# Seven-product blocks of a feed-forward layer in a new interleaving, with two sums per step left to accumulating transfers

## The chip, the cores and the metric

The kernel runs on one core of one Trainium2 chip. The time is device microseconds (us) of that core for one execution of the whole program; the kernel before has a median of 1907.07 us over three runs (1906.84 to 1908.11). The engines are named as the profile names them: PE (TensorE, matmuls), PEld (its weight loads), DVE (VectorE), ACT (ScalarE), POOL (GpSimd) and SP (SyncE, which here only issues transfers). Each engine takes its instructions strictly in the order in which they stand in its queue.

## The reference

Two layers work on 256 tokens of width 2048 in float32. Each layer has a first part (a projection, a gated unit, windowed attention and an output projection) and then a feed-forward part of width 5632:

```
D_FF = -(-8 * D_MODEL // (3 * 256)) * 256
...
        x = x + mixed @ w_out[l]
        h2 = rms_norm(x, norm2_g[l])
        x = x + (jax.nn.silu(h2 @ w_gate[l]) * (h2 @ w_up[l])) @ w_down[l]
```

Only the products with `w_gate` and `w_up` are touched by the change.

## The kernel before

**Exact products from split operands.** Every weight tile comes from HBM as float32, 128 partitions by 1024 elements (512 KB, a `raw` tile). `split2` (L117) makes two tiles of it: ACT casts it to `wh` (L123), and DVE subtracts that from the original, which gives `wl` (L124). `mm3` (L158) then issues three matmuls for each 128-row piece: high by high, high by low, low by high (L159 to L161). There are eight `raw` buffers, five of `wh` and four of `wl`. A `raw` buffer is free for the next load only when its last reader is done.

**Two streams of units.** The feed-forward part has eleven column blocks of 512. Ten of them (`S_BLOCKS`) are computed by `seven` (L338): the two token halves, two row parities of the weights and the pair (gate, up) form a two by two product, done with seven products in place of eight. One of these handles one `raw` tile and six matmuls at a time, called a half unit here. A block has four steps `i` over the rows, seven half units in each, so 28 half units. Beside them runs the plain stream: the eleventh block and the down projection, in full units of one `raw` tile and twelve matmuls (`unit`, L163). The loop at the end of `trunk` takes them in turn: it goes through 300 yields of the seven-product stream per layer and slips in the full units of the plain stream at an even rate, 83 of them over those yields, so about 8.3 full units for each block. The rest of the plain stream follows alone.

**The operands.** With B11 and B21 the two row parities of the gate weights and B12 and B22 those of the up weights, the seven products read: (one) B11; (two) B21, added to the same bank as one; (three) B22; (five) B11+B12; (six) B11+B12+B22, the tile `t2`; (seven) B12+B22; (four) `t2`+B21, added to the bank of seven. Five PSUM banks m0 to m4 hold the partial results of a block, and a few adds of 128x512 (m0, c21, c12, c22) join them.

**How the sums are made before.** In each step `i` the kernel loads B11, B12 and B22 together. DVE adds B12 onto B11 (L365) and makes `t2` (L366). B12+B22 is made for steps 0 and 2 by an accumulating transfer that POOL issues (L368: it reads B22 from HBM again and adds it onto the tile B12), for steps 1 and 3 by DVE (L372). B21 is added onto `t2` by another accumulating transfer (L374). In the second phase B21 is loaded once more as the operand of product two.

**What sets the order.** The Python code is traced in program order, and a list scheduler then decides in which order the instructions stand on each engine. It may move an instruction ahead of others of its engine when nothing it depends on forbids it; `tc.issue_after(x)` keeps instructions behind `x` on their engine. The order is fixed when the program is built.

Of the kernel before, what the change touches and what calls it, by code (L numbers as in the profile page):

```python
# [12 lines left out]
F32 = mybir.dt.float32  # L13
# [57 lines left out]
EXT_AT = (6.5, 8, 11, 13, 16, 18, 21.5, 24)  # L71
MASK_AFTER = ((5, 5), (4, 4))
GATE_LOAD = ((24, 29), (5, 15))
PARTS = (
    "a0 a0 a1 a1 s a0 a0 s a1 s a1 s s s b0 s b0 s b0 s b0 s b1 s b1 s b1 s b1 s b2 b2 b2 b2 b3 b3 b3 b3",
    "a0 a0 a1 a1 a0 a0 s a1 a1 s b0 b0 s b0 s b0 s s b1 s b1 s b1 s b1 s s b2 s b2 s b2 b2 s b3 b3 b3 b3",
# [14 lines left out]
def trunk(ctx, tc, x, xt, w_in, w_q, w_out, w_oa, w_uh, w_gate, w_up, w_down, sgu_w, sgu_g, consts,  # L91
# [66 lines left out]
    def mm3(acc, ah, al, wh, wl, first, last, again=False):  # L158
        nc.tensor.matmul(acc, ah, wh, start=first, stop=False, skip_group_check=again)  # L159
        nc.tensor.matmul(acc, ah, wl, start=False, stop=False, skip_group_check=again)  # L160
        nc.tensor.matmul(acc, al, wh, start=False, stop=last, skip_group_check=again)  # L161
# [171 lines left out]
    def seven(src, pairs, ext, out, end=lambda sg: None, soon=False, by_dma=(), put_off=False):  # L333
        bank = [pa.tile([P, NB], F32, tag="acc", name=f"m{i}") for i in range(5)]

        def s_unit(raw, m, i, op, first, last):
            wh, wl = split2(raw)
            for j in range(2):  # L338
                ah, al = (op(2 * i + j, h) for h in range(2))
                mm3(  # L340
                    bank[m], ah, al, wh[:, j, :], wl[:, j, :], first and j == 0,
                    last and j == 1, m in (0, 2),
                )
            tick(0.5)

        def a_op(k, t):
            return lambda p, h: pairs[p][:, h, k, t * P : (t + 1) * P]

        def e_op(n):
            return lambda p, h: ext[p][:, h, n, :]  # L350

        kept = []
        before = []
        for i in range(4):
            b11 = raw_load(src(0, 0, i))
            b12 = raw_load(src(0, 1, i))
            b22 = raw_load(src(1, 1, i))
            t2 = ap.tile([P, 2, NB], F32, tag="spt", name="t2", bufs=4)
            first, last = i == 0, i == 3
            s_unit(b11, 0, i, a_op(0, 0), first, last)  # L360
            yield
            if soon and first:
                s_unit(b22, 4, i, e_op(3), first, last)
                yield
            nc.vector.tensor_tensor(b11, b11, b12, ALU.add)  # L365
            nc.vector.tensor_tensor(t2, b11, b22, ALU.add)  # L366
            if i in by_dma:
                nc.gpsimd.dma_start(b12, src(1, 1, i), accum_op=ALU.add)  # L368
            s_unit(b11, 1, i, e_op(1), first, last)
            yield  # L370
            if i not in by_dma:
                nc.vector.tensor_tensor(b12, b12, b22, ALU.add)  # L372
            s_unit(t2, 3, i, e_op(2), first, last)
            anchor[0] = nc.gpsimd.dma_start(t2, src(1, 0, i), accum_op=ALU.add)  # L374
            yield
            if before:
                s_unit(*before.pop())
                yield
            if not (soon and first):
                s_unit(b22, 4, i, e_op(3), first, last)  # L380
                yield
            kept.append(t2)
            if put_off and i in by_dma and not last:
                before.append((b12, 2, i, e_op(0), first, last))
                continue
            s_unit(b12, 2, i, e_op(0), first, last)
            yield
        m0, c12, c21, c22 = (
            zp.tile([P, NB], F32, tag="z", name=v) for v in ("m0", "c12", "c21", "c22")
        )  # L390
        nc.scalar.copy(m0, bank[0])
        nc.vector.tensor_tensor(m0, bank[3], m0, ALU.add)
        yield

        def add(out, x, y):
            nc.vector.tensor_tensor(out, x, y, ALU.add)

        steps = {
            0: lambda: add(c21, bank[2], m0),
            1: lambda: (nc.scalar.copy(bank[2], c21), add(c12, bank[1], m0)),  # L400
            2: lambda: (add(c22, bank[1], c21), add(c12, bank[4], c12)),
            5: lambda: out(0, bank[0], m0, c12),
        }
        for i in range(8):
            if i < 4:
                s_unit(raw_load(src(1, 0, i)), 0, i, a_op(1, 0), False, i == 3)
            else:
                s_unit(kept[i - 4], 2, i - 4, a_op(1, 1), False, i == 7)
            yield
            steps.get(i, lambda: None)()  # L410
        later(1, lambda: out(1, bank[2], c21, c22))
        end([m0, c21])
        yield

    def seven_low(src, pairs, ext, done, tag="hT"):
        def half(raw, acc, op, i, first=False, stop=False):
            wh, wl = split2(raw)
            for j in range(2):
                ah, al = (op(2 * i + j, h) for h in range(2))
                mm3(  # L420
                    acc, ah, al, wh[:, j, :], wl[:, j, :], first and i + j == 0,
                    stop and i + j == 2, not first,
                )
            tick(0.5)

        def a_op(k, t):
            return lambda p, h: pairs[p][:, h, k, t * P : (t + 1) * P]

        def e_op(n):
            return lambda p, h: ext[p][:, h, n, :]  # L430

        def bank(name):
            return pa.tile([P, NB], F32, tag="acc", name=name)

        def held(name):
            return tp.tile([P, 2, NB], F32, tag=tag, name=name)

        x, y, s = [], [], []
        acc0 = bank("l0")
# [12 lines left out]
        nc.scalar.copy(acc1, acc0)  # L452
        for i in range(2):
            half(s[i], acc1, e_op(2), i, False, True)
            anchor[0] = nc.gpsimd.dma_start(s[i], src(1, 0, i), accum_op=ALU.add)
            yield
        mp = wp.tile([P, 2, NB], F32, tag="raw", name="mp", bufs=8)
        nc.scalar.copy(mp[:, 0], acc1)
        acc2 = bank("l2")
        for i in range(2):  # L460
            half(y[i], acc2, e_op(0), i, True, True)
            yield
        nc.scalar.copy(mp[:, 1], acc2)
        for i in range(2):
            half(raw_load(src(1, 0, i)), acc0, a_op(1, 0), i, False, True)
            yield
        done[0, 0](acc0, None)
        for i in range(2):
            half(x[i], acc1, e_op(1), i, False, True)
            yield  # L470
        done[1, 1](acc1, mp[:, 1])
        for i in range(2):
            half(s[i], acc2, a_op(1, 1), i, False, True)
            yield
        done[0, 1](acc2, mp[:, 0])
        for i in range(2):
            half(raw_load(src(1, 1, i)), acc1, e_op(3), i, False, True)
            yield
        done[1, 0](acc1, None)

    def q_product(lay, pairs, ext):
        q = {"k": 0}
        q["steps"] = seven(
            lambda r, c, i: w_q[lay, c, i, r], pairs, ext, lambda *a: q["out"](*a),
            soon=True, by_dma=range(4 if lay == 0 else 0),
        )
        return q

    def q_to(q, share):
# [32 lines left out]
    for lay in range(L):  # L522
# [526 lines left out]
        def act_later(b, sg, held=held, release=release):  # L1049
            for c in range(2):  # L1050
                def ready(c=c):
                    held.append((b, c, sg))
                    release()

                later(2 + c, ready)
# [3 lines left out]
            nc.vector.scalar_tensor_tensor(sg, c, nrstd2[t], sg, ALU.mult, ALU.mult)  # L1059

        def s_block(b, lay=lay, pairs2=pairs2, ext2=ext2, gated=gated, act_later=act_later):
            return seven(
                lambda r, c, i: (w_gate, w_up)[c][lay, b, i, r], pairs2, ext2, gated,
                lambda sg: act_later(b, sg), soon=b == S_BLOCKS[0], by_dma=(0, 2), put_off=True,
            )

        seven_done = [False]

        def s_stream(s_block=s_block):
            for b in S_BLOCKS:  # L1070
                yield from s_block(b)

        seeds = []
        left = [NFF]
# [230 lines left out]
```

## Time and profile before

| what | value |
|---|---|
| median of three runs | 1907.07 us |
| the profiled execution, its time | 1906.77 us |
| its span, first to last instruction | 1905.1 us |
| PE busy | 1892.9 us (99%) |
| DVE busy | 1745.5 us (92%) |
| ACT busy | 1374.7 us (72%) |
| POOL busy | 183.9 us (10%) |
| granted TensorE clock | 1.000 |

The first layer's seven-product stream runs from about 300 to 940 us of the span, the second's from about 1250 to 1855 us. The stretches from 370 to 860 us and from 1310 to 1800 us lie wholly inside, and each covers eight blocks. A row of the group view gives the line, engine, operation, output and inputs, shapes and count, then busy time and the mean of one in ns, then the idle time of the engine just before these instructions and what ended it. A row of the wait view gives the waiting engine and line, whom it waited for, the total in us, how many times and the longest. In the views PEld's waits are PE's: a matmul follows its weight load.

### The profile page before, as it was taken

How to read it: one execution, taken by the hardware profiler on the slowest of the kernel's cores; microseconds unless marked ns; L12 is line 12 of the kernel's file. 1: busy time of each engine (PE TensorE's matmuls, PEld its weight loads, DVE VectorE, ACT ScalarE, POOL GpSimd, SP SyncE). 2: the span in 40 equal slices, each digit the busy share in tenths (PEclk: the TensorE clock that was granted, in tenths of full speed). 3: DMA queues.
4: the chain of work that ended last, by engine and by line, in shares of the span. 5: the costliest groups of instructions: out<-in, count | busy, mean ns of one | idle time of the engine just before them, and what ended most of it. 6: DMA issues, size and time to landing. Idle time of an engine off the chain costs nothing.

```text
span 1905.1 us, 25218 instructions
## 1 busy us (share of the span) xinstructions
PE 1892.9 (99%) x8624; PEld 1544.2 (81%) x8624; DVE 1745.5 (92%) x1894; ACT 1374.7 (72%) x1860; POOL 183.9 (10%) x184
## 2 busy tenths in 40 slices
PE   9999999999999999999999999999999999999999
PEld 6887788888888888888888778888888888888887
DVE  7988989999999999999798888999999999999993
ACT  8668777677767776777776886766877677676774
POOL 0231001000100001000002200000000100010000
PEclk9999999999999999999999999999999999999999
DMA  9973668888977897889578648697789788888783
GB/s 356 261 284 133 194 202 243 248 247 276 271 238 245 270 290 228 243 261 290 185 217 291 191 153 237 212 280 224 233 282 288 227 254 264 270 249 251 249 277 110
DMA packets 129153, 463.12 MB, mean 243 GB/s; under 512 B 14336, under 2 KB 14720, under 8 KB 129024
## 3 DMA queue, kind: packets, MB, share of 16 engines
q1 hardware_dynamic: 105840, 378.54, 53.9%
q0 software_dynamic: 22464, 81.80, 23.7%
q8 instruction: 67, 1.10, 0.2%
q10 hardware_dynamic: 720, 1.18, 0.2%
q14 instruction: 62, 0.51, 0.1%
HBM read 459.36 MB, written 2.10 MB: 242 GB/s over the span
## 4 chain that ended last, share of the span: by engine, by line
PE 94%; ACT 2%; DVE 2%; issue 1%; DMA 0%; POOL 0%; SPq 0%; DVEq 0%; ACTq 0%; POOLq 0%
PE m L160 15%; PE m L159 15%; PE m L161 15%; PE dacc L160 11%; PE dacc L159 11%; PE dacc L161 11%; PE acc L160 4%; PE acc L161 3%; PE acc L159 3%; PE l L159 1%; PE l L160 1%; PE l L161 1%; PE ps_f L242 1%; PE ps_n L242 1%; DVE wl L124 1%
## 5 line engine op out<-in xcount | busy, mean ns | idle before, releaser
L123 ACT CAST wh<-raw 128x1024 fp32r<-128x1024 f32 (+1 forms) x794 | 814.0, 1050 | 366.5 <-DVE raw L365 165.7
L124 DVE TENSOR_TENSOR wl<-raw,wh 128x1024 fp32r<-128x1024 f32 (+1 forms) x794 | 943.9, 1217 | 83.0 <-issue 25.5
L159 PE MATMUL m<-wh,ext 128*128 128x512 f32 x704 | 276.7, 393 | 0.0
L160 PE MATMUL m<-wl,ext 128*128 128x512 f32 x704 | 275.0, 391 | 0.0
L161 PE MATMUL m<-wh,ext 128*128 128x512 f32 x704 | 274.4, 390 | 0.0
L160 PE MATMUL dacc<-wl,aT 128*128 128x512 f32 x624 | 243.5, 390 | 0.0
L159 PE MATMUL dacc<-wh,aT 128*128 128x512 f32 x624 | 243.0, 391 | 0.0
L161 PE MATMUL dacc<-wh,aT 128*128 128x512 f32 x624 | 242.9, 389 | 0.0
L124 DVE TENSOR_TENSOR wl<-t,wh 128x1024 fp32r<-128x1024 f32 x176 | 213.1, 1221 | 10.0 <-issue 5.2
L123 ACT CAST wh<-t 128x1024 fp32r<-128x1024 f32 x176 | 184.3, 1051 | 37.0 <-DVE t L366 14.1
L159 PE MATMUL m<-wh,hT 128*128 128x512 f32 x528 | 206.3, 391 | 0.0
L160 PE MATMUL m<-wl,hT 128*128 128x512 f32 x528 | 205.7, 390 | 0.0
L161 PE MATMUL m<-wh,hT 128*128 128x512 f32 x528 | 205.5, 389 | 0.0
L160 PEld LDWEIGHTS m<-wl,ext 128*128 128x128 f32 x704 | 132.2, 188 | 29.1 <-DVE wl L124 2.2
L159 PEld LDWEIGHTS m<-wh,ext 128*128 128x128 f32 x704 | 132.2, 188 | 27.6 <-ACT wh L123 0.8
L161 PEld LDWEIGHTS m<-wh,ext 128*128 128x128 f32 x704 | 132.1, 188 | 27.5
L159 PEld LDWEIGHTS dacc<-wh,aT 128*128 128x128 f32 x624 | 117.1, 188 | 25.0 <-ACT wh L123 0.7
L160 PEld LDWEIGHTS dacc<-wl,aT 128*128 128x128 f32 x624 | 117.2, 188 | 24.7 <-DVE wl L124 0.6
L161 PEld LDWEIGHTS dacc<-wh,aT 128*128 128x128 f32 x624 | 117.1, 188 | 24.2
L374 POOL DMA_DIRECT2D t<-in_w_gate_dram x80 | 69.1, 864 | 525.0 <-DVE wl L124 412.9
L161 PEld LDWEIGHTS m<-wh,hT 128*128 128x128 f32 x528 | 99.1, 188 | 20.6
L159 PEld LDWEIGHTS m<-wh,hT 128*128 128x128 f32 x528 | 99.1, 188 | 20.3
(212 smaller groups left out, 2907.5 us busy)
## 6 DMA issues: line engine op xcount, KB each, us to landing
raw<-in_w_gate_dram SPq DMA_DIRECT2D x176, 512.0 KB, 5.9
raw<-in_w_up_dram SPq DMA_DIRECT2D x176, 512.0 KB, 5.9
raw<-in_w_down_dram SPq DMA_DIRECT2D x176, 512.0 KB, 5.8
t<-in_w_gate_dram POOLq DMA_DIRECT2D x80, 512.0 KB, 7.7
raw<-in_w_in_dram SPq DMA_DIRECT2D x68, 512.0 KB, 6.7
raw<-in_w_out_dram SPq DMA_DIRECT2D x48, 512.0 KB, 4.3
raw<-in_w_up_dram POOLq DMA_DIRECT2D x40, 512.0 KB, 6.5
raw<-in_w_q_dram SPq DMA_DIRECT2D x32, 512.0 KB, 5.7
```

Source lines behind the costliest of these rows:

```text
L123: nc.scalar.copy(wh[:, j : j + step, :], src)
L124: last_wl[0] = nc.vector.tensor_tensor(wl[:, j : j + step, :], src, f(wh[:, j : j + step, :]), ALU.subtract)
L159: nc.tensor.matmul(acc, ah, wh, start=first, stop=False, skip_group_check=again)
L160: nc.tensor.matmul(acc, ah, wl, start=False, stop=False, skip_group_check=again)
L161: nc.tensor.matmul(acc, al, wh, start=False, stop=last, skip_group_check=again)
L242: nc.tensor.transpose(ps[:, j, t * P : (t + 1) * P], blocks[t][:, j * P : (j + 1) * P], ident)
L374: anchor[0] = nc.gpsimd.dma_start(t2, src(1, 0, i), accum_op=ALU.add)
```

## The change

A class `Lean` replaces `seven` for the ten feed-forward blocks of each layer; the query projection keeps `seven`. Its half units are the same seven products over the same four steps, but each product is a method that handles one step, and a table `LEAN` says when. Row m of the table has the places of product m+1 for the steps 0 to 3; block n is shifted by 28 places. The places of a block run to 37, so a block's last half units lie between the first ones of the next.

```diff
+LEAN = (
+    (0, 4, 8, 12), (24, 26, 27, 29), (6, 10, 14, 18), (30, 31, 33, 37), (7, 11, 15, 19),
+    (16, 20, 22, 23), (13, 17, 21, 25),
+)
...
+        def onto(self, dst, i):
+            anchor[0] = nc.gpsimd.dma_start(dst, self.src(0, 1, i), accum_op=ALU.add)
+
+        def one(self, i):
+            self.raw[1, i] = raw_load(self.src(0, 0, i))
+            self.half(1, self.raw[1, i], i)
+            self.onto(self.raw[1, i], i)
+
+        def three(self, i):
+            self.raw[3, i] = raw_load(self.src(1, 1, i))
+            self.half(3, self.raw[3, i], i)
+
+        def five(self, i):
+            self.half(5, self.raw[1, i], i)
+            self.t2[i] = ap.tile([P, 2, NB], F32, tag="spt", name="t2", bufs=4)
+            with tc.issue_after(last_wl[0].ins):
+                self.add(self.t2[i], self.raw[1, i], self.raw[3, i])
+            self.onto(self.raw[3, i], i)
+
+        def six(self, i):
+            if i == 0:
+                nc.scalar.copy(self.acc(3), self.bank[0])
+            self.half(6, self.t2[i], i)
...
+        def two(self, i):
+            b21 = raw_load(self.src(1, 0, i))
+            self.half(2, b21, i)
+            self.add(self.t2[i], self.t2[i], b21)
...
+                nc.scalar.copy(z["m0"], bank[3])
+            elif i == 1:
+                self.add(z["c21"], bank[2], z["m0"])
+            elif i == 2:
+                nc.scalar.copy(bank[2], z["c21"])
+                self.add(z["c12"], bank[1], z["m0"])
...
+    def lean_run(blocks):
+        steps = sorted(
+            (28 * n + LEAN[m][i], n, m, i) for n in range(len(blocks)) for m in range(7) for i in range(4)
+        )
+        for _, n, m, i in steps:
+            b = blocks[n]
+            (b.one, b.two, b.three, b.four, b.five, b.six, b.seven)[m](i)
+            yield
+            if m in (3, 5) and i == 3:
+                yield
...
         def s_stream(s_block=s_block):
-            for b in S_BLOCKS:
-                yield from s_block(b)
+            return lean_run([s_block(b) for b in S_BLOCKS])
```

B12 is no longer loaded as a tile. Two accumulating transfers per step add it onto B11 (after product one has been split) and onto B22 (after `t2` has been made). `t2` is still made by DVE. B21 is no longer added onto `t2` by a transfer that reads it a second time: DVE adds the tile that product two loads anyway. The bank of product six starts from a copy of m0 by ACT, in place of DVE's later add of the two banks (L392 before). Over both layers the program has 80 plain loads fewer on SP (176 of `w_up` become 96), 40 accumulating transfers more on POOL (120 become 160), 40 additions of 128x1024 fewer on DVE (the 120 of L365 and L372 go, 80 onto `t2` come), 20 additions of 128x512 fewer on DVE and 20 copies of 128x512 more on ACT. The number of matmuls is the same. Outside the two seven-product streams the order on PE is the same as before.

Three places show how the order moved. The first is DVE in the first layer around the transposes of a finished block (`aT` are the transposed results). `raw` are loaded tiles, the number tells the buffers of the text apart. Before:

```order
L1038 TENSOR_TENSOR aT_5033<-ps_f_5028,aT_5033 128x512
L365 TENSOR_TENSOR raw_5083<-raw_5083,raw_5085 128x1024
L366 TENSOR_TENSOR t2_5089<-raw_5083,raw_5087 128x1024
L124 TENSOR_TENSOR wl_5103<-raw_5083,wh_5102 128x1024
L372 TENSOR_TENSOR raw_5085<-raw_5085,raw_5087 128x1024
L1038 TENSOR_TENSOR aT_5070<-ps_f_5065,aT_5070 128x512
L124 TENSOR_TENSOR wl_5114<-t2_5089,wh_5113 128x1024
```

Now, at the same stage of a block of the first layer:

```order
L128 TENSOR_TENSOR wl_5682<-raw_5537,wh_5681 128x1024
L453 TENSOR_TENSOR t2_5691<-raw_5537,raw_5651 128x1024
L128 TENSOR_TENSOR wl_5697<-t2_5516,wh_5696 128x1024
L1141 TENSOR_TENSOR aT_5648<-ps_f_5643,aT_5648 128x512
L128 TENSOR_TENSOR wl_5707<-raw_5560,wh_5706 128x1024
L128 TENSOR_TENSOR wl_5719<-raw_5716,wh_5718 128x1024
L453 TENSOR_TENSOR t2_5516<-t2_5516,raw_5841 128x1024
L128 TENSOR_TENSOR wl_5737<-raw_5734,wh_5736 128x1024
```

Before, DVE made three sums in a row for one step. Now it makes one, `t2_5691`; and the sum onto `t2_5516`, which reads the tile `raw_5841` of product two, stands behind `t2_5691` with four rows between, thirteen DVE rows ahead of the split of that same tile (`wl_5844`).

The second place is SP at the loads that belong to these rows. Before:

```order
L112 DMA raw_5083<-in_w_gate_dram 128x1024
L112 DMA raw_5085<-in_w_up_dram 128x1024
L112 DMA raw_5087<-in_w_up_dram 128x1024
L112 DMA raw_5130<-in_w_down_dram 128x1024
L112 DMA raw_5178<-in_w_gate_dram 128x1024
```

Now:

```order
L116 DMA raw_5560<-in_w_up_dram 128x1024
L116 DMA raw_5578<-in_w_down_dram 128x1024
L116 DMA raw_5619<-in_w_gate_dram 128x1024
L116 DMA raw_5651<-in_w_up_dram 128x1024
L116 DMA raw_5663<-in_w_down_dram 128x1024
L116 DMA raw_5716<-in_w_down_dram 128x1024
L116 DMA raw_5734<-in_w_up_dram 128x1024
L116 DMA raw_5779<-in_w_down_dram 128x1024
L116 DMA raw_5823<-in_w_down_dram 128x1024
L116 DMA raw_5841<-in_w_gate_dram 128x1024
```

Before, the three tiles of a step come together. Now they come one by one. When DVE has made `t2_5691` and so given back `raw_5537`, the tiles 5560, 5619, 5651, 5716, 5734, 5779 and 5823 of this list are still wanted or still to come, seven of the eight buffers, and `raw_5841` is the next to be loaded.

More of the change, by code (lines that the diff above doesn't have):

```diff
@@ L413, in seven, with __init__, a_op, e_op @@
         yield
+    class Lean:
+        def __init__(self, src, pairs, ext, out, end=lambda sg: None):
+            self.src, self.out, self.end = src, out, end
+            self.bank, self.raw, self.t2, self.z = {}, {}, {}, {}
+            def a_op(k, t):
+                return lambda p, h: pairs[p][:, h, k, t * P : (t + 1) * P]
+            def e_op(n):
+                return lambda p, h: ext[p][:, h, n, :]
+            self.home = {
+                1: (0, a_op(0, 0)), 2: (0, a_op(1, 0)), 3: (4, e_op(3)), 4: (2, a_op(1, 1)),
+                5: (1, e_op(1)), 6: (3, e_op(2)), 7: (2, e_op(0)),
+            }
+        def acc(self, m):
+            if m not in self.bank:
+                self.bank[m] = pa.tile([P, NB], F32, tag="acc", name=f"m{m}")
+            return self.bank[m]
+        def half(self, n, raw, i):
+            m, op = self.home[n]
+            wh, wl = split2(raw)
+            first, last = n in (1, 3, 5, 7) and i == 0, i == 3
+            for j in range(2):
+                ah, al = (op(2 * i + j, h) for h in range(2))
+                mm3(
+                    self.acc(m), ah, al, wh[:, j, :], wl[:, j, :], first and j == 0,
+                    last and j == 1, m in (0, 2, 3),
+                )
+            tick(0.5)
+        def add(self, out, x, y):
+            nc.vector.tensor_tensor(out, x, y, ALU.add)
+        def onto(self, dst, i):
[17 more added lines that the diff above has]
+            self.half(6, self.t2[i], i)
+        def seven(self, i):
+            self.half(7, self.raw[3, i], i)
+        def two(self, i):
+            b21 = raw_load(self.src(1, 0, i))
+            self.half(2, b21, i)
+            self.add(self.t2[i], self.t2[i], b21)
+            z, bank = self.z, self.bank
+            if i == 0:
+                for v in ("m0", "c12", "c21", "c22"):
+                    z[v] = zp.tile([P, NB], F32, tag="z", name=v)
+                nc.scalar.copy(z["m0"], bank[3])
[4 more added lines that the diff above has]
+                self.add(z["c12"], bank[1], z["m0"])
+            else:
+                self.add(z["c22"], bank[1], z["c21"])
+                self.add(z["c12"], bank[4], z["c12"])
+        def four(self, i):
+            self.half(4, self.t2[i], i)
+            z, bank = self.z, self.bank
+            if i == 0:
+                self.out(0, bank[0], z["m0"], z["c12"])
+            elif i == 3:
+                later(1, lambda: self.out(1, bank[2], z["c21"], z["c22"]))
+                self.end([z["m0"], z["c21"]])
@@ L415, in seven_low @@
+    def lean_run(blocks):
+        steps = sorted(
+            (28 * n + LEAN[m][i], n, m, i) for n in range(len(blocks)) for m in range(7) for i in range(4)
+        )
+        for _, n, m, i in steps:
[4 more added lines that the diff above has]
+                yield
     def seven_low(src, pairs, ext, done, tag="hT"):
@@ L482, in q_product @@
         q = {"k": 0}
[L483 to L486, printed above, removed]
+        args = (lambda r, c, i: w_q[lay, c, i, r], pairs, ext, lambda *a: q["out"](*a))
+        q["steps"] = seven(*args, soon=True, by_dma=range(4 if lay == 0 else 0))
         return q
@@ L1061, in s_block @@
         def s_block(b, lay=lay, pairs2=pairs2, ext2=ext2, gated=gated, act_later=act_later):
-            return seven(
+            return Lean(
                 lambda r, c, i: (w_gate, w_up)[c][lay, b, i, r], pairs2, ext2, gated,
-                lambda sg: act_later(b, sg), soon=b == S_BLOCKS[0], by_dma=(0, 2), put_off=True,
+                lambda sg: act_later(b, sg),
             )
```

## The prediction

> **What bounds the kernel now.** I read the engines' busy time in the seven-product stretches first, then PE's waits there, then what DVE and the transfers do under them.
>
> The windows view: the first layer's start of this part, then 370 to 860 us (first layer) and 1310 to 1800 us (second), each eight blocks long:
>
> ```profile
> core 0: us, PE busy (x) PEld busy (x) DVE busy (x) ACT busy (x) POOL busy (x), PEclk, DMA share, GB/s
> 252.00:300.00 48.00, 48.00 (x224) 39.70 (x224) 42.58 (x64) 32.44 (x53) 2.46 (x3) 1.00 0.66 205
> ...
> 370.00:860.00 490.00, 490.00 (x2191) 403.95 (x2190) 470.80 (x441) 349.35 (x409) 40.63 (x47) 1.00 0.84 258
> ...
> 1310.00:1800.00 490.00, 490.00 (x2189) 403.73 (x2188) 470.80 (x442) 351.94 (x411) 41.53 (x48) 1.00 0.84 258
> ```
>
> PE is the bound: 490.00 of 490. DVE stands close behind with 96%, ACT has 71%, the transfers 84%. A block takes 490/8 = 61.25 us, a matmul 490/2191 = 0.224 us, so a half unit (six) 1.34 us and a full unit 2.68 us. Since the number of matmuls stays, the change can gain only what PE still waits. A busy PE may hide waits, so I take them from the wait view of PE's weight loads, 300 to 940 us and then 1250 to 1860 us:
>
> ```profile
> PEld ps_f L242 <- DVE aT L1038: 1.5, 4, 0.4
> PEld m L160 <- DVE wl L124: 1.0, 4, 0.4
> PEld dacc L159 <- ACT wh L123: 0.4, 1, 0.4
> PEld m L159 <- ACT wh L123: 0.3, 1, 0.3
> PEld dacc L160 <- DVE wl L124: 0.3, 1, 0.3
> PEld ps_f L242 <- DVE c L1059: 0.3, 1, 0.3
> ```
>
> ```profile
> PEld ps_f L242 <- DVE aT L1038: 1.4, 4, 0.4
> PEld m L160 <- DVE wl L124: 0.8, 3, 0.4
> PEld m L159 <- ACT wh L123: 0.5, 2, 0.3
> PEld dacc L159 <- ACT wh L123: 0.4, 1, 0.4
> PEld dacc L160 <- DVE wl L124: 0.3, 1, 0.3
> PEld ps_f L242 <- DVE c L1059: 0.2, 1, 0.2
> ```
>
> Here is the whole prize. The splits (wl and wh rows) make PE wait 2.0 us in each layer, 4.0 in all; the transposes that wait for DVE (ps_f rows) 1.8 and 1.6, 3.4 in all. Together 7.4 us, 0.39% of the time. No removal of DVE work can give more than this.
>
> **The change part by part. DVE's work.** DVE's groups between 370 and 860 us, eight blocks:
>
> ```profile
> L124 DVE TENSOR_TENSOR wl<-raw,wh 128x1024 fp32r<-128x1024 f32 x224 | 265.4, 1220 | 10.8 <-issue 4.1 <-ACT wh L123 4.0 <-PE dacc L160 1.0
> L124 DVE TENSOR_TENSOR wl<-t,wh 128x1024 fp32r<-128x1024 f32 x63 | 76.1, 1221 | 4.2 <-issue 2.2 <-ACT wh L123 1.4
> L365 DVE TENSOR_TENSOR raw<-raw 128x1024 f32<-128x1024 f32 x32 | 39.2, 1224 | 0.9
> L366 DVE TENSOR_TENSOR t<-raw 128x1024 f32<-128x1024 f32 x32 | 39.1, 1223 | 0.9
> L372 DVE TENSOR_TENSOR raw<-raw 128x1024 f32<-128x1024 f32 x15 | 18.3, 1217 | 0.0
> L392 DVE TENSOR_TENSOR m<-m,m 128x512 f32<-128x512 f32 x8 | 5.5, 686 | 0.6 <-PE m L161 0.6
> ```
>
> Gone are L365, L372 and L392: 39.2 + 18.3 + 5.5 = 63.0 us. Four additions of B21 per block come, 32 in this stretch; the trace has none, but L366 is the same operation on the same kinds of tile: 39.1 us. Net 23.9 us less of 470.8. DVE's idle time goes from 490 - 470.8 = 19.2 to 43.1 us, from 2.4 to 5.4 us per block: 96% busy becomes 91%, and the reserve doubles.
>
> **ACT and PSUM.** ACT gets 20 copies, of the kind of these rows of the page:
>
> ```profile
> L400 ACT COPY m<-c 128x512 f32<-128x512 f32 x22 | 12.9, 588 | 5.3 <-DVE c L396 5.1
> L391 ACT COPY m<-m 128x512 f32<-128x512 f32 x22 | 12.7, 576 | 0.0
> ```
>
> 20 x 0.58 = 11.6 us over 1,220 us, hidden in ACT's idle time (140.65 of 490 us); without that cover it would cost these 11.6 us. The chain from product seven's last step over c21 (0.69, as L392) and its copy (0.59) to product four has, by the order, five half units between on PE at the narrowest, 6.7 us. With three splits queued ahead on DVE (3.66) it needs 4.9, so I put it at nothing.
>
> **The transfers.** The DMA view of 370 to 860 us, and SP's own waits there:
>
> ```profile
> q1 hardware_dynamic: 27691, 100.85, 54.3%
> q0 software_dynamic: 6912, 25.17, 29.4%
> ...
> raw<-in_w_down_dram SPq DMA_DIRECT2D x65, 512.0 KB, 5.7
> raw<-in_w_up_dram SPq DMA_DIRECT2D x64, 512.0 KB, 6.0
> raw<-in_w_gate_dram SPq DMA_DIRECT2D x63, 512.0 KB, 6.3
> t<-in_w_gate_dram POOLq DMA_DIRECT2D x31, 512.0 KB, 7.6
> raw<-in_w_up_dram POOLq DMA_DIRECT2D x16, 512.0 KB, 6.7
> ```
>
> ```profile
> SPq L112 <- DVE wl L124: 409.7, 192, 6.6
> ```
>
> A load costs 54.3% of 490 us over 192, 1.39 us of all 16 engines; an accumulating transfer 29.4% of 490 over 47, 3.07 us. A block loses four of the first and gains two of the second: +0.6 us, 84% becomes 85%. So the transfers get no relief though they move fewer bytes. POOL is busy 40.63 of 490 us and takes two more issues per block easily. The accumulated sums are read six or seven places of the table later. At the narrowest, four half units and two full ones lie between on PE, 4 x 1.34 + 2 x 2.68 = 10.7 us; they land in 6.7 to 7.6 us, and with ACT's cast are in time:
>
> ```profile
> L123 ACT CAST wh<-raw 128x1024 fp32r<-128x1024 f32 x223 | 228.5, 1052 | 107.4 <-DVE raw L365 65.2 <-PE dacc L161 22.5 <-PE m L161 10.2
> ```
>
> 7.6 + 1.05 is under 10.7. I put this at nothing; the third rival below has what it costs otherwise. Only the first block of a layer has nothing interleaved: there product five of step 0 follows its product one after three half units and one full unit, 6.7 us, where landing and cast need 7.8 to 8.7. That is 1.1 to 2.0 us short, once per layer, and the lead of the splits may cover it: bounds 0 and 4.0 us for both layers; I take 0.7, nearer to nothing, since PE is busy 48.00 of 48 us from 252 to 300 us, where that block starts, and DVE there only 42.58: the splits can be ahead.
>
> **The new wait.** The sum onto `t2` on DVE now reads a loaded tile long before that tile's own split, and nothing queued behind it on DVE (the next splits, and PE after them) can pass. SP waits 192 times for 192 loads above: every load goes out when a buffer comes free. In the piece of order shown, `raw_5841` can go out when `t2_5691` is done, and DVE has four rows until it needs it: three splits and a 128x512 operation as in L392, 3 x 1.22 + 0.69 = 4.3 us. The load takes 6.3 (the w_gate row). DVE then stands still for 2.0 us. Through the order of a layer, sixteen of the forty such sums have 3.7 to 6.1 us of DVE rows between the release and the sum, 82.5 us in all; the others have 7.3 or more. At 6.3 us they cost 16 x 6.3 - 82.5 = 18.3 us of DVE per layer, 1.8 per block. The order before has no such place: DVE has at least 8.5 us of rows between release and first use.
>
> DVE's stall is PE's only where it exceeds the splits' lead. There are four `wl` buffers, so DVE can be three units ahead of the one on PE, 4.0 us in half units; a mean stall of 18.3/16 = 1.1 us fits in. For the few of 2 us and more at a moment of little lead I put 1.0 us over both layers; bounds are 0 and what the rival below gives.
>
> **The sum.** DVE's free reserve is 5.4 - 1.8 = 3.6 us per block where it was 2.4. The waits for splits (4.0) could go wholly or stay; I take half off, -2.0. The waits for transposes (3.4) hang on DVE too, but also on the one bank that is handed back and forth; half, -1.7. New stalls +1.0, first blocks +0.7: -2.0. The profiled execution took 1906.77 us, 1.7 outside its span of 1905.1; it becomes 1904.8, and from the median of 1907.07, 0.3 above it, **1905.1 us**.
>
> **The rivals.** *The load decides (slower).* If the loads behind the sixteen sums take 7.6 us, as the slower accumulating transfers do, DVE stalls 16 x 7.6 - 82.5 = 39.1 us per layer, 3.9 per block, and its free reserve falls to 1.5, less than before. The seven sums with 4.9 us of rows or less then stall 2.7 to 3.9 us, more than two half units of lead: 0.6 x 3 + 1.2 = 3.0 us of PE per layer, and with the old waits staying and a second stall before the lead has come back I count 6 us: 1913. It decides from landings of about 7.2 us on, where stalls (16 x 7.2 - 82.5 = 32.7) eat the 30 us per layer that were won. For it: the transfers stay at 85%, and an accumulating one is in flight most of the time (8 x 7 us of 61). Against: loads now go out singly, not by three, and rows of stages without accumulating transfers are quicker:
>
> ```profile
> raw<-in_w_out_dram SPq DMA_DIRECT2D x48, 512.0 KB, 4.3
> ```
>
> [...]
>
> *All waits go (faster).* If DVE keeps the reserve and the landings stay under 5.2 us, the mean of the sixteen, the 7.4 us go but for a little: 1900 to 1903. For it: the wait rows nearly all name DVE. Against: a transposed tile's bank must come back within two half units whatever the reserve.
>
> *The sums come too late (no relief).* If accumulating transfers land in twice their 6.7 us, ACT's casts stand for them and push every split: 13.4 + 1.05 against 10.7 us, 3.7 us, which is over two half units of lead by 1.0; with ten such blocks in each layer some 10 to 20 us, 1922 at the middle. The rows speak against it.
>
> **Chances and range.** A measurement tells about 0.2%, 3.8 us, from no change. Small gain or none, 55%, own range 1902 to 1909; all waits go, 22%; the load decides, 19%; sums late, 4%. Faster than 1903.3: nearly all of the second and 7 of the first, 27%. Slower than 1910.9: 15 of the third, 4 of the fourth and 1 of the first, 20%. Between: 53%. The range of eight in ten reaches from 1900.5, a tenth below it where nearly all waits go, to 1912.5 inside the slower rival.
>
> **What will show it.** Right: the 370 to 860 us window again has 490 us PE with DVE near 450 us busy; the `wl` rows lose their PE waits; DVE rows of the sum onto `t2` show about 18 us of waiting for w_gate loads per layer, PEld less than 5 us of waits in all. Wrong: PE waiting for `wl` more than 2 us per layer (the load rival), ACT's casts waiting for accumulating transfers (the third), w_gate landings over 7.2 us, or a difference that lies outside the two streams, where the order on PE is unchanged.

## The result, and the profile after

The changed kernel takes 1928.83 us (median; 1926.76 to 1931.53) against 1907.59 us beside it on the same chip: a ratio of 1.0112, with a 95% interval of 1.0095 to 1.013. It is slower by 21 us where 2 us less were forecast, and 16 us beyond the price of the rival "the load decides". The profiled execution took 1928.26 us, its span is 1926.5 us.

The windows view of the changed kernel, over the same two stretches as in the prediction:

```profile
core 0: us, PE busy (x) PEld busy (x) DVE busy (x) ACT busy (x) POOL busy (x), PEclk, DMA share, GB/s
370.00:860.00 490.00, 483.96 (x2156) 396.88 (x2155) 438.41 (x413) 354.66 (x412) 51.92 (x60) 1.00 0.86 237
1310.00:1800.00 490.00, 483.10 (x2151) 395.99 (x2151) 439.02 (x409) 353.86 (x408) 53.73 (x62) 1.00 0.86 236
```

DVE has the relief that was worked out (470.80 became 438.41), the transfers stand at 86% as expected, and PE is no longer busy throughout. The better measure is its count of matmuls: 2156 and 2151 where 2191 and 2189 were, 73 fewer. At 0.224 us each that is 16.4 us of these 980, and by that rate an estimated 21 us over both streams (1260 us): about the whole loss.

PE's waits, 300 to 940 us and then 1260 to 1880 us (lines have moved: L128 is the split that was L124, L1141 the DVE half of a transposed tile that was L1038):

```profile
PEld m L164 <- DVE wl L128: 5.6, 8, 1.4
PEld ps_f L246 <- DVE aT L1141: 4.4, 3, 1.7
PEld dacc L164 <- DVE wl L128: 3.4, 4, 1.2
PEld dacc L163 <- ACT dacc L1210: 1.0, 2, 0.5
```

```profile
PEld m L164 <- DVE wl L128: 5.0, 8, 1.3
PEld ps_f L246 <- DVE aT L1141: 3.9, 3, 1.9
PEld dacc L164 <- DVE wl L128: 3.0, 3, 1.2
PEld dacc L163 <- ACT dacc L1210: 1.5, 2, 1.2
```

With the one small row of each view that is left out here (0.3 and 0.2) these are 14.7 and 13.6 us, 28.3 in all against 7.4 before: 20.9 us more, about the loss again. Nearly all rows name DVE, an engine with less work than before. So the next view is what DVE itself waits for (first layer, 370 to 860 us), and the same for ACT; the last line is DVE's row for the whole span, both layers:

```profile
DVE t L453 <- DMA raw<-in_w_gate_dram: 25.1, 10, 4.3
DVE wl L128 <- ACT wh L127: 11.2, 16, 1.3
```

```profile
ACT wh L127 <- DMA raw<-in_w_up_dram: 16.1, 11, 2.4
```

```profile
DVE t L453 <- DMA raw<-in_w_gate_dram: 53.2, 24, 4.3
```

The waits for transfers are new. L453 is the sum of B21 onto `t2`, which stands ahead of the split of the same tile: DVE waits there for the load, ten times, 2.5 us on average. Of the 53.2 us, 42.3 fall on the first sum of a block (15 of the 20 blocks), 10.9 on the fourth. And ACT's casts wait for `w_up`, in every case for an accumulating transfer that has not landed; of 37.5 us over both layers 34.5 are for the second one of a step. The DMA view of the stretch:

```profile
raw<-in_w_gate_dram SPq DMA_DIRECT2D x64, 512.0 KB, 5.7
raw<-in_w_up_dram POOLq DMA_DIRECT2D x60, 512.0 KB, 8.3
```

The median of the `w_gate` loads did not rise (6.3 before). The place that the prediction took as its example, the sum that reads `raw_5841`, shows why that helps nothing. Three pieces of the timeline, SP, DVE and, of PE's weight loads, those that waited (start, length, instruction, and in brackets the idle time before it; SP's row merges three loads, the first is that of `raw_5841`):

```profile
626.06 5.05 SPq L116 DMA_DIRECT2D raw<-in_w_gate_dram  x3
```

```profile
624.78 1.22 DVE L453 TENSOR_TENSOR t<-raw 128x1024 f32<-128x1024 f32 x1
625.91 1.22 DVE L128 TENSOR_TENSOR wl<-t,wh 128x1024 fp32r<-128x1024 f32 x1
627.79 0.69 DVE L1141 TENSOR_TENSOR aT<-ps_f,aT 128x512 fp32r<-128x512 f32 x1 [0.66 <-ACT aT L1140]
628.40 2.35 DVE L128 TENSOR_TENSOR wl<-raw,wh 128x1024 fp32r<-128x1024 f32 x2
634.80 1.23 DVE L453 TENSOR_TENSOR t<-t,raw 128x1024 f32<-128x1024 f32 x1 [4.05 <-DMA raw<-in_w_gate_dram]
635.95 2.35 DVE L128 TENSOR_TENSOR wl<-raw,wh 128x1024 fp32r<-128x1024 f32 x2
```

```profile
637.22 0.19 PEld L164 LDWEIGHTS m<-wl,ext 128*128 128x128 f32 x1 [1.41 <-DVE wl L128]
640.62 0.19 PEld L164 LDWEIGHTS m<-wl,ext 128*128 128x128 f32 x1 [0.78 <-DVE wl L128]
644.03 0.19 PEld L164 LDWEIGHTS dacc<-wl,aT 128*128 128x128 f32 x1 [0.80 <-DVE wl L128]
```

The sum that frees the buffer ends at 626.0, SP issues the load in the same instant, DVE works off the four rows that were counted, and then it stands until the load has landed at 634.8: 8.7 us after its issue, not 6.3. The split behind it comes 1.41 us late for PE, and two more splits within 7 us come 0.78 and 0.80 us late. DVE stood 4.05 us, and PE lost 3.0 us by it. The lead, that is how far DVE's splits are ahead of PE, took up only the rest.

### The profile page after: what moved, and what is told of

It is laid out like the page before. It is cut to its first block, busy times and chain, and to the rows that moved or that the text cites. A ratio compares the mean times of both kernels' runs of the same rounds, so it can differ in the third digit from the quotient of the medians.

```text
span 1926.5 us, 25414 instructions
## 1 busy us (share of the span) xinstructions
PE 1900.0 (99%) x8624; PEld 1545.9 (80%) x8624; DVE 1684.4 (87%) x1834; ACT 1399.8 (73%) x1880; POOL 217.8 (11%) x224
## 4 chain that ended last, share of the span: by engine, by line
PE 87%; DVE 5%; issue 3%; ACT 2%; DMA 2%; POOL 0%; SPq 0%; DVEq 0%; ACTq 0%; POOLq 0%
PE m L164 13%; PE m L163 13%; PE m L165 13%; PE dacc L164 10%; PE dacc L163 10%; PE dacc L165 10%; PE acc L164 3%; PE acc L163 3%; PE acc L165 3%; DVE wl L128 2%; DMA raw<-in_w_up_dram 2%; PE l L163 1%; PE l L164 1%; PE l L165 1%; PE ps_f L246 1%
## 5 line engine op out<-in xcount | busy, mean ns | idle before, releaser
L127 ACT CAST wh<-raw 128x1024 fp32r<-128x1024 f32 (+1 forms) x794 | 822.4, 1050 | 346.4 <-PE dacc L165 168.2
L128 DVE TENSOR_TENSOR wl<-raw,wh 128x1024 fp32r<-128x1024 f32 (+1 forms) x794 | 949.6, 1218 | 114.1 <-ACT wh L127 43.3
L456 POOL DMA_DIRECT2D raw<-in_w_up_dram x160 | 138.6, 869 | 1074.4 <-DVE wl L128 395.5
L128 DVE TENSOR_TENSOR wl<-t,wh 128x1024 fp32r<-128x1024 f32 x176 | 212.3, 1219 | 7.4 <-ACT wh L127 4.2
L453 DVE TENSOR_TENSOR t<-t,raw 128x1024 f32<-128x1024 f32 x80 | 97.4, 1221 | 53.6 <-DMA raw<-in_w_gate_dram 53.2
L164 PEld LDWEIGHTS m<-wl,hT 128*128 128x128 f32 x528 | 99.2, 188 | 22.3 <-DVE wl L128 2.3
```

Of the source, the lines that this page charges most:

```text
L127: nc.scalar.copy(wh[:, j : j + step, :], src)
L128: last_wl[0] = nc.vector.tensor_tensor(wl[:, j : j + step, :], src, f(wh[:, j : j + step, :]), ALU.subtract)
L456: anchor[0] = nc.gpsimd.dma_start(dst, self.src(0, 1, i), accum_op=ALU.add)
```

## The experiments

Three theories. A: DVE stands at the hoisted sum until its load has landed, and the splits behind it come late. B: the accumulating transfers land late for ACT's casts, and the splits come late through them. C: the new sequence of half units and banks makes PE wait. A kernel with lines added has its transposed tile at L1142 or L1145. Times are medians; the kernel before took 1907.7 to 1908.4 us beside them.

### One sum or all sums behind their splits

All four sums of a block:

```diff
             self.half(2, b21, i)
-            self.add(self.t2[i], self.t2[i], b21)
+            with tc.issue_after(last_wl[0].ins):
+                self.add(self.t2[i], self.t2[i], b21)
```

> Every sum of B21 onto t2 is kept behind the split of the same tile on DVE; the accumulating transfers, the banks and the table stay. Theory A (DVE stands at the hoisted sum until its w_gate tile has landed, and the splits behind it come late for PE): DVE's 25 us of waits for w_gate loads between 370 and 860 us fall below 4, PE's waits fall from 14.7 to 4 or 5 us per layer, time 1905 to 1909. Theory B (ACT's casts wait for the accumulating transfers, 16.1 us in that stretch, and the splits come late through them): both stay, time 1924 to 1930. Theory C (the new sequence of half units and banks itself makes PE wait): 1924 to 1930.

Only that of step 0, and then only those of steps 1 to 3 (`i > 0` in place of `i == 0`):

```diff
             self.half(2, b21, i)
-            self.add(self.t2[i], self.t2[i], b21)
+            if i == 0:
+                with tc.issue_after(last_wl[0].ins):
+                    self.add(self.t2[i], self.t2[i], b21)
+            else:
+                self.add(self.t2[i], self.t2[i], b21)
```

> Only the sum of step 0 of each block is kept behind its split; those of steps 1 to 3 may still be hoisted. In the changed kernel the first sum of a block carries 24.2 of the 29.8 us that the sums wait in the first layer. Theory A: most of the loss goes, 1909 to 1915, unless the sum of step 1, now the first of its block, takes over the wait (then 1918 to 1926). Theories B and C: 1924 to 1930.

> The complement: the sums of steps 1 to 3 are kept behind their splits, the first of each block stays hoisted. Theory A: the first sums still wait about 3 us each, seven or more times per layer, time 1922 to 1929. Theories B and C: 1924 to 1930 as well, so this run tells only together with the one before.

| kernel | us | ratio to before (95%) |
|---|---|---|
| changed kernel | 1928.83 | 1.0112 (1.0095 to 1.013) |
| first sum behind | 1910.68 | 1.0017 (1.0008 to 1.0027) |
| sums 1 to 3 behind | 1931.60 | 1.0122 (1.0104 to 1.0141) |
| all four behind | 1917.53 | 1.005 (1.0035 to 1.0065) |

One instruction per block, put behind its split, takes 18 of the 21 us back; the other three in the same way take nothing back, and end above the 1922 to 1929 that were expected. PE's waits with the first sum behind, 300 to 940 us, and DVE's wait for loads, 370 to 860 us and then over the whole span:

```profile
PEld ps_f L246 <- DVE aT L1145: 3.8, 3, 2.3
PEld dacc L164 <- DVE wl L128: 1.1, 1, 1.1
```

```profile
DVE t L453 <- DMA raw<-in_w_gate_dram: 8.2, 6, 2.4
DVE t L453 <- DMA raw<-in_w_gate_dram: 14.8, 13, 2.4
```

DVE's wait went from 25.1 to 8.2 us (from 53.2 to 14.8 over the span) and the `wl` rows all but vanished. Theory C falls with this as the main cause: sequence and banks are unchanged. B cannot be the main cause either, since the transfers, their issue and their use are unchanged; the casts' waits for them even fell, from 37.5 to 22.2 us over the span, so a part of those waits was itself brought about by DVE's standing. That all four behind is worse than one was not expected (1905 to 1909). There DVE has no wait for a load left, yet PE waits 7.1 us in the first layer, 0.3 of them in a row left out here:

```profile
PEld ps_f L246 <- DVE aT L1142: 4.7, 3, 1.9
PEld m L164 <- DVE wl L128: 2.1, 4, 1.4
```

The hoisting had also spread the four sums. Kept behind, they stand between the splits of product two, which follow each other at 24, 26, 27 and 29 in the table. That this crowding is what costs there is argued from the order, not shown.

### The sum without its load

```diff
-            self.add(self.t2[i], self.t2[i], b21)
+            self.add(self.t2[i], self.t2[i], self.t2[i])
```

> The changed kernel, but the hoisted sums add t2 to itself in place of the loaded tile (left out of the computation: B21 in product four). DVE does the same work in nearly the same places, the loads and accumulating transfers stay. Theory A in its narrow form (the wait for the tile is the loss): no waits of DVE for w_gate, PE's waits at 4 to 6 us per layer, 1905 to 1911. If the place of the sum among the splits is the loss: 1922 to 1930. Theory B: 1922 to 1930.

This leaves B21 out of product four. 1910.34 us, ratio 1.0012 (1.0002 to 1.0022). DVE does the same number of additions in nearly the same places, hoisted as before, and 18 us are back. So it is neither the work nor its place but the wait for the tile.

### No accumulating transfers

```diff
             self.half(1, self.raw[1, i], i)
-            self.onto(self.raw[1, i], i)
...
-            self.onto(self.raw[3, i], i)
```

> Left out of the computation: the two accumulating transfers of each step (B12 is added to nothing, products five, six and seven read what is there). The hoisted sums stay. 80 times 3.07 us of all 16 DMA engines go per layer. Theory A: with no accumulating transfer in flight the w_gate loads land in about 4.5 us in place of 7 to 9 and the hoisted sums wait less than 5 us per layer: 1900 to 1906. Theory B: the same, since the casts no longer wait. Theory C: 1924 to 1930.

1904.73 us, ratio 0.9985 (0.9975 to 0.9994): the only kernel here that is faster than before, and it leaves work out (B12 in products five, six and seven). DVE's instructions stand in the very order of the changed kernel, the sums hoisted as there. Its DMA view and DVE's wait for loads, 370 to 860 us:

```profile
raw<-in_w_down_dram SPq DMA_DIRECT2D x65, 512.0 KB, 3.4
raw<-in_w_gate_dram SPq DMA_DIRECT2D x64, 512.0 KB, 3.4
```

```profile
DVE t L453 <- DMA raw<-in_w_gate_dram: 1.5, 2, 0.9
```

Without accumulating transfers a `w_gate` load lands in 3.4 us (median), and the hoisted sums wait 1.5 us; with two per step it takes 5.7 us, and the sums wait 25.1 us in the same stretch. So the same hoisted sums hurt only together with the accumulating transfers. Even here the gain is only 3 us. PE is busy 490.00 of 490 us with 2197 and 2196 matmuls, against 2191 and 2189 before: 13 matmuls, 2.9 us of these 980. The 7.4 us of waits that the prediction called the whole prize brought about 3 when nearly all of them were gone.

### Buffers

Nine buffers for loaded tiles need room; one `wh` tile was given up. The control gives it up without the ninth buffer.

```diff
-        raw = wp.tile([P, 2, NB], F32, tag="raw", name="raw", bufs=8)
+        raw = wp.tile([P, 2, NB], F32, tag="raw", name="raw", bufs=9)
...
-        wh = wp.tile([P, 2, NB], F32R, tag="wh", name="wh", bufs=5)
+        wh = wp.tile([P, 2, NB], F32R, tag="wh", name="wh", bufs=4)
```

> The changed kernel with nine buffers for loaded tiles in place of eight (and four for wh in place of five, to make room). Loads go out when a buffer comes free; SP issues 158 loads in 490 us, one in 3.1 us, so one buffer more lets a load go about 3 us earlier, where the first sums wait 1.9 to 4.3. Theory A with too few buffers as its root: DVE's 25.1 us of waits for w_gate fall to 5 to 10, time 1908 to 1917. Theory B (accumulating transfers late for ACT) : 1924 to 1930, since their issue and their use stay. If the load queue merely fills the ninth buffer with loads of other tiles that stand earlier in SP's order, the first sums wait as before: 1922 to 1930.

> Control for the run with nine buffers: the changed kernel with four wh tiles in place of five, eight buffers for loaded tiles as before. If the four wh alone cost what that run cost (1947): 1940 to 1955, with most of the loss outside the two streams; then the ninth buffer neither helped nor hurt. If the ninth buffer was at fault: 1927 to 1932. If the ninth buffer helped as theory A says and four wh hid it: above 1955.

1947.28 us with nine buffers, 1990.08 us without. My expectation for the first was wrong: I had not reckoned with what four `wh` cost. Against its control the ninth buffer is worth 43 us. DVE's wait for loads without and with it:

```profile
DVE t L453 <- DMA raw<-in_w_gate_dram: 35.4, 13, 5.3
```

```profile
DVE t L453 <- DMA raw<-in_w_gate_dram: 15.3, 8, 3.5
```

Matmuls in the two windows rise from 2079 and 2075 to 2159 and 2150. So a free buffer does shorten these waits. (With four `wh` the scheduler also puts DVE's instructions in another order, so these two are compared with each other and not with the changed kernel.) What nine buffers with five `wh` would do stays open, since there is no room for both.

With the first sum behind its split as well, and nine buffers:

> The sum of step 0 behind its split and nine buffers (four wh). Control for the run without late reads, and the question whether buffers matter once the first sum is out of the way: DVE's 8.2 us of waits for w_gate between 370 and 860 us should go; 1906 to 1910 if they were part of what is left above 1904.7, 1910 to 1912 if what is left is the accumulating transfers or the transposes.

1922.99 us, so neither of the two outcomes: DVE's waits for loads fell from 8.2 to 2.0 us, but four `wh`, and the other order that they bring, cost more than that, and mostly outside the two windows, which have 2182 and 2175 matmuls where the first sum behind alone has 2179 and 2184.

### Late accumulating transfers

First try, on the kernel with nine buffers and the first sum behind:

```diff
             self.half(1, self.raw[1, i], i)
-            self.onto(self.raw[1, i], i)
...
-            self.onto(self.raw[3, i], i)
+            self.onto(self.raw[1, i], i)
...
             self.half(7, self.raw[3, i], i)
+            self.onto(self.raw[3, i], i)
```

> The sum of step 0 behind its split, nine buffers, four wh; both accumulating transfers of a step are issued only after the last reading of their tile, so that no cast reads an accumulated tile (left out of the computation: B12 in products five, six and seven). The load on the DMA engines is the same, a tile is held longer by a transfer, which the ninth buffer makes good. If casts waiting for accumulating transfers are what keeps the kernel above 1904.7: ACT's waits for them are gone and the time is 1904 to 1907, below the run with nine buffers alone. If it is the load of the transfers on the DMA engines, or the transposes: the same as that run within 1.5 us.

2018.97 us, 96 us slower than its control, and far from both outcomes that were expected. (It leaves B12 out of products five, six and seven.) ACT's waits are gone as meant, but the tiles are held until the transfer has landed, and the ninth buffer does not make that good: loads go out later still, and DVE stands at the sums for 45.0 us in 370 to 860, where its control has 2.0:

```profile
DVE t L453 <- DMA raw<-in_w_gate_dram: 45.0, 15, 6.9
```

For B this says nothing; it is theory A at a larger dose. The second try gives the second transfer of a step more time, on the kernel with the first sum behind:

```diff
-    (0, 4, 8, 12), (24, 26, 27, 29), (6, 10, 14, 18), (30, 31, 33, 37), (7, 11, 15, 19),
-    (16, 20, 22, 23), (13, 17, 21, 25),
+    (0, 4, 8, 12), (24, 26, 27, 29), (6, 10, 13, 17), (30, 31, 33, 37), (7, 11, 15, 19),
+    (16, 20, 21, 23), (14, 18, 22, 25),
```

> The sum of step 0 behind its split, and in the table product seven one place later for steps 0 to 2, with products three (steps 2, 3) and six (step 2) one place earlier to make room: seven half units between products five and seven in place of six. If casts that wait for the second accumulating transfer of a step (18.9 of the 22 us in both streams of the run with the first sum behind) are what is left: those waits fall below 10 us and the time is 1906 to 1909.5. If not: 1909.5 to 1913.

1908.06 us, ratio 1.0000 (0.999 to 1.0009), 2.6 us below the kernel with the first sum behind alone. The casts' waits for the second transfer (summed from each cast's idle time) fell from 18.9 to 6.8 us over both streams, those for the first rose from 3.4 to 8.5, and 4.1 us are new, for plain `w_up` loads. In all they went only from 22.2 to 19.4. The later place of product seven, put on the sum without its load:

> The hoisted sums read no load (left out of the computation: B21 in product four) and product seven stands one place later. If the wait for the load and the late second accumulating transfer are all that separates the changed kernel from 1904.7 but for the transposes: 1905 to 1908, below the 1910.3 of the first alone. If the second has no part of its own: 1909 to 1912.

1908.22 us, ratio 0.9999 (0.9989 to 1.0009), 2.1 us below the sum without its load alone, just above what was expected. Twice the changed table took off some 2 us, and the intervals of each pair touch or overlap at their edges. That it did so by sparing the casts their waits is not shown: here these waits rose in all, from 23.2 to 25.5 us (9.8 of them for plain loads), and the table moves products three and six as well. B as a small second cause stays open.

### What is left, and where the sums belong

Two sums behind, each sum behind product two's previous split (with product seven later), and the transposes moved, once the second pair alone (on the first sum behind), once both (with product seven later):

```diff
-            if i == 0:
+            if i < 2:
```

> The sums of steps 0 and 1 behind their splits, those of 2 and 3 may be hoisted: between the run with one (1910.7, DVE waits 8.2 us for w_gate in 490) and the run with all four (1917.5, none). If the remaining 8.2 us of DVE waits matter: 1906 to 1910. If what costs in the run with all four is that the sums crowd between product two's splits: 1911 to 1917.

```diff
             if i == 0:
-                with tc.issue_after(last_wl[0].ins):
-                    self.add(self.t2[i], self.t2[i], b21)
-            else:
-                self.add(self.t2[i], self.t2[i], b21)
+                self.mark = last_wl[0].ins
+            with tc.issue_after(self.mark):
+                self.add(self.t2[i], self.t2[i], b21)
+            self.mark = last_wl[0].ins
```

> Product seven one place later as in the run e10, and each sum kept behind product two's previous split (the first behind its own): no sum stands more than four rows ahead of its tile's split. If the waits of the still hoisted sums (6.7 us in 490) are worth something: 1904 to 1908. If sums that crowd at the end of the block, where the splits of products two and four follow each other, cost what the run with all four behind showed: 1912 to 1918.

```diff
-                later(2 + c, ready)
+                later(2 + 2 * c, ready)
...
-                later(2 + c, ready)
+                later(3 + c, ready)
```

> The sum of step 0 behind its split, and the second pair of transposes of a finished block one full unit later (two units after the first in place of one). If the waits for the handed-back bank (ps_f for aT, 3.8 us in the first layer, about 7 in both) are what is left: 1904 to 1907. If the waits just show up elsewhere: 1909 to 1912. Theory B for what is left (late accumulating transfers) says 1909 to 1912.

> As e10, with both transposes of a finished block one full unit later. If the waits for the handed-back bank (3.6 and 4.1 us per layer, all of PE's waits there) come from where the transposes stand: 1902 to 1906. If they only move or new waits take their place, as when only the second pair was moved: 1907 to 1914.

None helps: 1924.19, 1913.36, 1915.1 and 1923.83 us. The first, third and fourth lie outside all that was expected; the second falls in the range for crowded sums. With two sums behind, those of steps 2 and 3 now mostly stand 8 to 12 rows ahead of their splits. DVE's wait for loads over the whole span and a piece of its timeline:

```profile
DVE t L453 <- DMA raw<-in_w_gate_dram: 28.3, 13, 4.1
```

```profile
326.59 1.23 DVE L453 TENSOR_TENSOR t<-t,raw 128x1024 f32<-128x1024 f32 x1 [0.47 <-DMA raw<-in_w_gate_dram]
327.74 1.22 DVE L128 TENSOR_TENSOR wl<-t,wh 128x1024 fp32r<-128x1024 f32 x1
332.76 1.22 DVE L453 TENSOR_TENSOR t<-t,raw 128x1024 f32<-128x1024 f32 x1 [3.81 <-DMA raw<-in_w_gate_dram]
```

The wait has not gone but moved: 28.3 us where one sum behind has 14.8, and 26.7 of them on the second sum of a block in order of time. The single wait of 3.81 us, with one split between it and another sum, makes PE wait 2.8 us. Each sum in its turn leaves DVE no wait for a load, but the sums again stand close together, and PE's waits are 12.2 us over both streams where the version with product seven later has 7.7. The transposes were most of PE's waits in that version (3.3 and 3.0 us). With the second pair alone moved, the row is gone and splits wait in its place, in each layer once for 2.9 us. With both moved, the bank comes back through ACT's half of the transposed tile, which is queued behind a cast, and that cast waits 4.0 us for a `w_down` load; the row grows from 3.3 to 7.5 us:

```profile
PEld ps_f L246 <- DVE aT L1145: 7.5, 4, 3.8
```

No version here that computes everything beats the kernel before; the best, with the first sum behind and product seven later, equals it.

## Why the prediction was wrong

**What bounds the kernel: right.** PE is the bound, the loss lies in the two streams, and PE's wait rows account for 20.9 of its 21.2 us. The size of the prize was too high: with nearly every wait gone the time fell by 3 us, not 7.4. The 7.4 us were waits of the weight loads, while the windows of before had PE busy throughout (490.00 of 490 us); so a part of them was likely covered by matmuls still running.

**DVE's work, ACT, the transfers' load: right.** DVE 438 us where 447 were worked out, some of it work that had not come by 860 us since the stream runs later; transfers 86% for 85%. But the relief was worth nothing: PE waits on when a split comes, not on how much DVE has to do.

**The step that failed: the new wait, "+1.0".** Place and mechanism were right, and it is the mechanism of the rival "the load decides", with 19%. The term was mis-sized: put at 1.0, it measured about 18 of the 21 us, by the two runs that took the wait for the tile away. Its size was wrong in three steps of the working; the second and third weigh most, since DVE's stalls themselves were 53.2 us over both layers where 36.6 were worked out.

1. "At 6.3 us they cost 16 x 6.3 - 82.5 = 18.3 us": the length of these loads was taken from the median of all `w_gate` loads. That median is 5.7 now, but the loads behind the fifteen first sums that waited took 5.2 to 9.1 us, with a median of 7.9 (the example 8.7), and each of them had two or three accumulating transfers in flight beside it. Without accumulating transfers the median of all is 3.4.
2. "a mean stall of 18.3/16 = 1.1 us fits in": the stalls do not spread over sixteen sums. In eight blocks ten of them wait 2.5 us on average, the longest 4.3, and the first of a block carries most: put behind its split, it alone took back 18 us.
3. "DVE can be three units ahead of the one on PE, 4.0 us in half units": that is what the buffers allow, not what DVE always has. Nine first sums stood 3.06 to 4.32 us; within the next 10 us PE waited for splits between nothing (twice, the longest stall among them) and 3.0 us (twice). At the example it was 1.41 + 0.78 + 0.80 of 4.05.

The rival had the right loads, and they landed past its threshold of 7.2 us. It even put DVE's stalls too high, at 39.1 us per layer where 26.6 were measured on average, and still its price of 1913 was 16 us short: it too let the lead cover nearly all of them.

**Waits for splits (-2.0) and transposes (-1.7): wrong in sign.** Splits went from 4.0 to 17.0 us, transposes from 3.4 to 8.8 (with the small rows), and 2.5 us for a copied bank (`dacc`) are new. For the splits the stalls are the cause, as shown above. For the transposes they are at most a part: the six waits of that row (8.3 us) all stand 6 to 9 us ahead of a first sum that waits, not behind it, and with no load read 5.4 us stay; without accumulating transfers it is 1.2. In all six the new ACT copy of m0 (L476, 0.58 us), which the prediction hid in ACT's idle time, stands one cast ahead of ACT's half of the transposed tile. No run moves that copy, so its part is open. Moving the transposes did not make the time shorter.

**Accumulating transfers read six or seven places later, "at nothing": not quite.** 10.7 us against 7.6 + 1.05 was reckoned with the landing times of before. The median rose to 8.3 us, and the second transfer of a step is issued only when DVE, itself late, has made `t2`. Casts waited 16.1 us in the first stretch. That is the sign named for the third rival, in a mild form; what it costs PE is not shown. The two runs with the changed table took off some 2 us, which bounds it only if the table acts through these waits.

**Too few buffers.** With four `wh` the ninth buffer for loaded tiles cut DVE's waits for loads from 35.4 to 15.3 us (370 to 860 us); with five no run shows it.

## What to carry to other kernels

An operation that a scheduler hoists ahead on an in-order queue brings its load's landing with it (at the example 8.7 us from issue to landing, of which DVE stood 4.05): before trusting spare time on that engine, look at each place where a moved instruction reads a fresh load, and compare the rows between the buffer's release and that reading with the landing time of loads issued at that moment, not with the median. An engine's busy share going down says nothing about when its results arrive: here DVE went from 470.80 to 438.41 us of 490, and PE's waits from 7.4 to 28.3 us. And count the lead from the trace (stall less the waits that follow it) at several places, not from the number of buffers: here stalls of about 4 us cost PE anything from nothing to 3.0 us.

## What the runs showed of the hardware

A PE wait cost twice here. The windows view of the run with both transposes later, around its longest wait, 3.84 us:

```profile
684.00:688.00 4.00, 1.15 (x6) 0.59 (x4) 1.06 (x2) 1.74 (x3) 0.00 (x0) 0.92 1.06 292
688.00:692.00 4.00, 3.43 (x10) 2.91 (x11) 3.38 (x4) 2.27 (x3) 0.00 (x0) 0.50 0.99 346
692.00:696.00 4.00, 4.00 (x14) 3.18 (x13) 2.01 (x2) 1.05 (x1) 0.00 (x0) 0.72 0.58 200
696.00:700.00 4.00, 4.00 (x19) 3.31 (x18) 3.12 (x4) 1.16 (x2) 0.87 (x1) 1.00 0.54 144
```

The granted clock (the number after POOL's) is 0.50 in the 4 us behind the wait and 1.00 again from 696 us on. PE goes on at 688.6; at the 19 matmuls of the last row the 7.4 us to 696 would hold 35, and they hold 24. By an estimate from these counts that is another 11 x 0.21 = 2.3 us. It also came behind a shorter wait; this one, 2.50 us, is from the run with four `wh`, and behind it the windows view of the same place:

```profile
1504.29 0.19 PEld L164 LDWEIGHTS m<-wl,ext 128*128 128x128 f32 x1 [2.50 <-DVE wl L128]
```

```profile
1504.69:1508.10 3.41, 3.41 (x10) 2.67 (x9) 3.41 (x4) 1.04 (x1) 0.86 (x1) 0.50 0.17 34
```

It does not follow from such a wait every time. In the run with the second pair of transposes moved, PE is busy 5.56 us of 684 to 692 and 5.54 us of 1631 to 1639, so the gaps are alike; the granted clock stays 1.00 up to 696 at the first, and is 0.65 from 1635 to 1639 and 0.92 in the 4 us after that at the second. What decides it is not shown. In the changed kernel the granted clock is 1.00 in both streams (300 to 940 and 1260 to 1880 us), where its longest wait is 1.9 us, so its 21 us hold none of this. But part of what the moved transposes (0.50 above), two sums behind (0.69 from 334 to 338 us, 0.59 from 1288 to 1292) or four `wh` (0.50 above) lost is clock.

A plain 512 KB `w_gate` load landed in 3.4 us (median) with no accumulating transfer about and 5.7 us with two per step, at 53% and 86% of the DMA engines' time (370 to 860 us); the fifteen loads behind first sums that waited, each with two or three accumulating transfers in flight, took 7.9 us (median).
